# Moving eight of layer B's adaLN columns from the K/V products into the SSD output product

## The chip, the cores and the metric

The kernel runs on one core of one Trainium2 chip. The metric is the device time of one execution in microseconds (us); lower is better. A time is the median of several executions. One further execution is recorded by the hardware profiler; the profile and all queries of the trace come from that one.

## The reference, cut to what matters

The program is a two-layer decoder trunk for 256 tokens of width 2048, in float32. Layer A is a Mamba-2 (SSD) mixer, layer B a dilated-window attention. Each layer is

```
shift, scale, gate = split(silu(c) @ ada_w[layer] + ada_b[layer])       # adaLN, three vectors of 2048
h = x * (1 + scale) + shift
x = layer_norm(alpha * x + (1 + gate) * mixer(h)) * ln_g + ln_b
```

For layer A the mixer ends in `y @ out_w` with `y` 256 x 4096 and `out_w` 4096 x 2048: the "output product" below. After layer A the shared keys and values `x @ kv_w` (2048 x 6144) are made: the "K and V products". Layer B then forms its `h` with its own shift and scale, which need `c` alone, and multiplies it with `b_in_w`.

`ada_w` is 2048 x 6144 per layer. The kernel cuts it into 48 columns per layer (16 for each of shift, scale and gate), each a block of 128 x 2048 float32, 1 MB. A column is worked off without TensorE: the block is loaded and one VectorE instruction multiplies it with silu(c), laid out on every partition, and sums each row.

## The kernel before, in words

**Products.** Every large product is cut into weight pieces of 128 x 1024 float32 (512 KB). SP issues the load of a piece (`load_piece`, L93, tile `raw`, six buffers). ScalarE (ACT) rounds it to the fast matmul type (`split`, L99, tile `whi`, four buffers), VectorE (DVE) subtracts that from the original (L101, tile `wlo`, four buffers), and TensorE (PE) multiplies both parts with the split activations. So each piece passes SP, ACT, DVE and PE, and each engine works off its own instructions strictly in the order in which they were written into its queue.

**Output product** (L734 to L754). `tm_chunk` runs four chunks n = 0 to 3 of 512 output columns, 16 pieces each, for two halves of the tokens (b = 0, 1). Each matmul is one of L173 (high part by high part), L174 (low part of the weights) and L175 (low part of the activations). At the end of a chunk `residual` (L696 to L698, DVE) multiplies the sum by the gate, adds alpha * x and takes LayerNorm statistics, for each half. Chunk 3 also splits four pieces of the first V product (`first_weights`) in between. After it follow the LayerNorm's moments (L703 to L710) and normalisation (L720, ACT), the transposes (L766), and the copies of the transposed tiles (L769 on ACT, L770 on DVE).

**K and V products** (L808 to L821). First a V chunk (wv[4], 8 pieces), then twelve K tiles by `cm_wide` (4 pieces each, 48 in all; matmuls L149 and L152; each tile's sum is copied out by L156 on ACT and L157 on DVE), then three V chunks (wv[1], wv[3], wv[5], 24 pieces). Then comes layer B's `h` (L828, L829, L197, L198), the attention bias (load L835, use L868), the LayerNorm rows (tile `pT`, load L63, use L848) and layer B's input product.

**Columns in the background.** `queue(pool, cols)` (L267) puts one job per column into a list: a job issues the load of the next column (L244 on SP, tile `araw`, two buffers) and the dot of its own (L251 on DVE). `background(n, every)` (L106), called after each piece, adds n to a counter and runs a job for each full `every`. So a rate (1, 4) is one column for four pieces, (1, 2) one for two, (2, 5) two for five. `drain` (L279) runs what is left. Layer B's 48 columns are the list `cols1`: first 32 of scale and shift in turn, then 16 of gate. `pin` holds a dot back until a given earlier DVE instruction has been issued. The scheduler that writes the queues takes instructions in the order of the program, with each engine's readiness, so a job's place on DVE isn't exactly the place where it was called.

In before, the first 11 columns run in chunks 1 to 3 of the output product, at (1, 4) from 44 calls of `background` (the last four pieces of chunk 3 are split together and call it not). The other 37 run in the K and V products at (1, 2).

Of the kernel before, what the change touches and what calls it, by code (L numbers as in the profile page):

```python
# [21 lines left out]
KT = D // P  # L22
# [27 lines left out]
def trunk(ctx, tc, xT, x, c, par, cst, bias, lnrow, ada, wdt, win, wxs, wout, wk, wv, wbin, wbout, out):  # L50
# [11 lines left out]
    def bcast(dst, src, off=0):  # L62
        nc.sync.dma_start(dst, bass.AP(tensor=src.tensor, offset=src.offset + off,  # L63
                                       ap=[[0, P], [1, dst.shape[-1]]]))
# [22 lines left out]
    def rows(t, b):  # L87

        return t.rearrange("(j r) n -> r j n", r=2)[b]
# [42 lines left out]
    def cm_quad(src, ahi, alo, rate=(0, 1), k0=0):  # L132
        ps = acc_pair()
        for q in range(k0 // 2, KT // 2):
            cm_piece(src, q, ps, ahi, alo, k0=k0)
            background(*rate)
        return ps

    def cm_wide(src, dst, rate=(0, 1), moving=None):

        both, high = moving or (lambda kt: xp[:, kt], lambda kt: xhi[:, kt, :])
        ps = acc_pair()
        for q in range(KT // 4):
            hi, lo = (t.rearrange("p k n -> p (k n)").rearrange("p (k n) -> p k n", k=4)
                      for t in split(load_piece(src[q])))
            for k in range(4):
                kt = 4 * q + k
                for n in range(2):
                    T.matmul(ps[n], hi[:, k, n * P:n * P + P], both(kt), start=kt == 0, stop=False,  # L149
                             skip_group_check=True)  # L150
                for n in range(2):
                    T.matmul(ps[n][:, 0, :], lo[:, k, n * P:n * P + P], high(kt), start=False, stop=kt == KT - 1,  # L152
                             skip_group_check=True)
            background(*rate)
        for n in range(2):
            S.activation(dst[:, n, :], ps[n][:, 1, :], AF.Copy)  # L156
            V.tensor_tensor(dst[:, n, :], ps[n][:, 0, :], dst[:, n, :], op=ALU.add)  # L157

    def tiles(ps):
        return [ps[n // 2][:, n % 2, :] for n in range(4)]  # L160
# [17 lines left out]
    def tm_pair():  # L178
        return [mm.tile([P, 512], F32, name="acc") for _ in range(2)]

    def tm_chunk(src, ahi, alo, nk=KT, rate=(0, 1), k0=0, pre=None, split_end=0):

        ps = tm_pair()
        n = nk // 2 - split_end
        for q in range(k0 // 2, n):
            if pre:
                pre(q)
            tm_piece(src, q, ps, ahi, alo, k0, nk)
            background(*rate)
        held = [(q, split(load_piece(src[q]))) for q in range(n, nk // 2)]  # L190
        for b in range(2):
            for q, w in held:
                tm_mults(q, w, ps, ahi, alo, k0, nk, (b,))
        return ps
# [41 lines left out]
    def shift(i, kt):  # L236
        return mod[i][:, kt, 0:1]

    def scale(i, kt):
        return mod[i][:, kt, 1:2]  # L240

    def ada_load(pool, layer, kind, ct):
        raw = pool.tile([P, D], F32, name="araw", bufs=2)
        nc.sync.dma_start(raw, ada[layer, KIND.index(kind), ct])  # L244
        return raw

    def ada_dot(layer, kind, ct, raw):

        j = KIND.index(kind)
        with tc.issue_after(pin[0]) if pin[0] is not None else ExitStack():  # L250
            V.scalar_tensor_tensor(raw, raw, 1.0, cb_, op0=ALU.mult, op1=ALU.mult,  # L251
                                   accum_out=mod[layer][:, ct, j:j + 1])
# [14 lines left out]
    def queue(pool, cols):  # L267

        loaded = [ada_load(pool, *cols[0])]

        def step(i):
            raw = loaded.pop(0)
            if i + 1 < len(cols):
                loaded.append(ada_load(pool, *cols[i + 1]))
            ada_dot(*cols[i], raw)

        jobs.extend(lambda i=i: step(i) for i in range(len(cols)))

    def drain():  # L279
        while jobs:  # L280
            jobs.pop(0)()
# [8 lines left out]
    with ExitStack() as cA:  # L290
# [14 lines left out]
        with ExitStack() as cS:  # L305
# [38 lines left out]
            def xs_wide(g):  # L344

                xs[g] = p0.tile([P, 4, L], F32, name="xs")
                for w in range(2):
                    t = xs[g][:, 2 * w:2 * w + 2, :]
                    cm_wide(wxs[2 * g - 4 + w], t, rate=R, moving=(lambda kt: hp[:, :, kt, :], hh_))
                    for n in range(2):  # L350
                        conv(t[:, n, :], 4 * g + 2 * w + n, t[:, n, :])

            def product(kind, g, pre=None):
# [7 lines left out]
                if kind == "z":  # L361
                    ps = tm_chunk(src, hh_, hl_, rate=R, k0=k0, pre=pre)
                    if g not in sz:
# [5 lines left out]
                    return  # L369
                ps = cm_quad(src, hhi, hlo, rate=R, k0=k0)  # L370
                t = tiles(ps)
# [9 lines left out]
            with ExitStack() as c0:  # L381
# [42 lines left out]
                for row in ("b4:0. b6:0. h z2:0. b2:0 x1:0 h", "b2:1. x1:1. z1:0 z1:1. z4:0 h h",  # L424
# [3 lines left out]
                    for w in row.split():  # L428
                        if w == two:
                            n = -2 if sum(o[0] == -2 for o in order) == sum(o[0] == -1 for o in order) else -1  # L430
# [98 lines left out]
            px = pe = cS.enter_context(tc.tile_pool(name="px", bufs=2, reuse_waits="tile"))  # L529
            R = (1, 10)  # L530

# [133 lines left out]
        pn = cA.enter_context(tc.tile_pool(name="pn", bufs=1, reuse_waits="tile"))  # L665
# [47 lines left out]
        cols1 = [(1, kind, kt) for kt in range(KT) for kind in ("scale", "shift")] + \  # L713
# [19 lines left out]
        jobs.append(lambda: gate_out(0))  # L733
        for n in range(4):  # L734
            ps = tm_chunk(wout[n], lambda kt: yhi[kt // 16][:, kt % 16, :], lambda kt: ylo[kt // 4][:, kt % 4, :],
                          nk=2 * KT, rate=(1, 4) if n else (1, 2),
                          pre={0: y_ahead, 3: first_weights}.get(n), split_end=4 if n == 3 else 0)
            if n == 0:
                drain()
                pin[0] = latest[-3].ins  # L740
                state[0] = 0
                queue(pn, cols1[:11])
            if n == 3:
                drain()
            gt = pn.tile([P, 512], F32, name="gt")
            bcast(gt, gated[0], 512 * n)
            for b in range(2):
                xr = pn.tile([P, 512], F32, name="xr", bufs=2)
                nc.sync.dma_start(xr, rows(x, b)[:, 512 * n:512 * n + 512])
                residual(n, ps[b], b, (gt, u[b][:, 512 * n:512 * n + 512]), xr)  # L750
                if n == 3:
                    norm.append(moments(b, 4))
                    normalise(b, 0, 256)
                    normalise(b, 256, 512)  # L754
# [29 lines left out]
    with ExitStack() as cL:  # L784
        pl = cL.enter_context(tc.tile_pool(name="pl", bufs=3))

        vps = [tm_pair(), tm_pair()]
        for b in range(2):
            for kt in range(4):
                tile4 = x_tile(kt, (b,))  # L790
            for n in range(1, 4):
                normalise(b, 512 * n, 512 * n + 512)
            for i, w in enumerate(first_v):
                if b and i == 2:
                    x_tile(4)
                    x_tile(5)
                tm_mults(i // 2, w, vps[i % 2], hx, lx, 0, KT, (b,))
        for q in range(2, KT // 2):
            if q < KT // 2 - 1:
                x_tile(2 * q + 2)  # L800
                x_tile(2 * q + 3)
            for j in range(2):
                w = split(load_piece(wv[2 * j][q]), after=tile4.ins if q == 2 else None)
                tm_mults(q, w, vps[j], hx, lx, 0, KT, range(2))
        for g in range(2):
            evict_v(0, g, vps[g])

        R = (1, 2)  # L808
        pin[0] = latest[-1].ins
        with tc.issue_after(tile4.ins):  # L810
            state[0] = 0
            queue(pl, cols1[11:])
            jobs.append(lambda: gate_out(1))
            evict_v(0, 2, tm_chunk(wv[4], hx, lx, rate=R))
            for hq in range(2):
                for g in range(NG):
                    kv[hq, g] = place(3 + 3 * hq + g, [P, 4, L])
                    for w in range(2):
                        cm_wide(wk[2 * (2 * g + hq) + w], kv[hq, g][:, 2 * w:2 * w + 2, :], rate=R)
            for g in range(NG):  # L820
                evict_v(1, g, tm_chunk(wv[1 + 2 * g], hx, lx, rate=R))  # L821
            drain()
            late = latest[-1].ins

        ada_bias(1, slice(0, KT), slice(0, 2))
        for kt in range(KT):
            t = pl.tile([P, L], F32, name="htmp")
            S.activation(t, xhi[:, kt, :].bitcast(F32), AF.Identity, bias=shift(1, kt), scale=scale(1, kt))  # L828
            V.scalar_tensor_tensor(t, xlo[:, kt, :].bitcast(F32), scale(1, kt), t, op0=ALU.mult, op1=ALU.add)  # L829
            split_act(xhi[:, kt, :], xlo[:, kt, :], t)  # L830
# [7 lines left out]
    R = (0, 1)  # L838
# [269 lines left out]
```

## Time and profile before

| | us |
|---|---|
| median of 3 runs | 1255.48 |
| lowest, highest | 1254.13, 1258.44 |
| the profiled execution | 1254.31 |
| its span in the trace | 1252.5 |
| mean granted TensorE clock | 0.998 of full |

In the rows of the profile a group reads: line, engine, operation, output <- input, shape, count, then busy time, mean ns of one, idle time ahead of it and what ended most of that. In a row of a timeline the first number is the start and the second the duration, both in us; the bracket at the end holds the engine's idle time before it and the instruction that ended it. A row of the chain has start, time and what was then last. PEld is the loading of weights into TensorE, which overlaps the matmuls.

### The profile page before, as it was taken

What the parts mean: (1) busy time and instruction counts of PE and PEld (TensorE: products, weight loads), DVE (VectorE), ACT (ScalarE), POOL (GpSimd) and SP (SyncE); (2) the same over time, 40 slices, a digit from 0 to 9 for tenths busy, and PEclk for the clock granted to TensorE, in tenths of its full rate; (3) what the DMA queues carried; (4) which work ended last, traced back from release to release, by engine and by line L of the source; (5) the groups of instructions that cost most, each with busy time, mean ns of one, the idle gap of its engine ahead of it and who ended that gap; (6) DMA issues with size and microseconds to landing.
All of it is one profiled execution on the core that took longest, in us unless ns stands there. A gap on an engine that the chain in (4) does not pass through costs nothing.

```text
span 1252.5 us, 18746 instructions
## 1 busy us (share of the span) xinstructions
PE 1218.5 (97%) x7086; PEld 1042.7 (83%) x7086; DVE 1032.4 (82%) x1466; ACT 702.1 (56%) x1039; POOL 0.2 (0%) x4
## 2 busy tenths in 40 slices
PE   4999999999999999999999999999999999999997
PEld 4989998898888878788888788888888888888886
DVE  6999986999987989899777778879888866758777
ACT  3655577869588789653444444434445644445631
POOL 0000000000000000000000000000000000000000
PEclk9999999999999999999999999999999999999999
DMA  9999977677556546699898569989998774464741
GB/s 381 422 421 423 420 252 261 225 274 286 201 169 225 171 159 202 223 328 358 335 323 298 174 192 383 363 315 344 364 389 309 229 248 136 132 203 120 228 177 67
DMA packets 80586, 335.88 MB, mean 268 GB/s; under 512 B 9104, under 2 KB 9328, under 8 KB 67696
## 3 DMA queue, kind: packets, MB, share of 16 engines
q1 hardware_dynamic: 80496, 334.69, 73.9%
q8 instruction: 55, 0.90, 0.3%
q14 instruction: 35, 0.29, 0.1%
HBM read 332.47 MB, written 2.18 MB: 267 GB/s over the span
## 4 chain that ended last, share of the span: by engine, by line
PE 86%; DVE 5%; DMA 5%; issue 2%; ACT 1%; SPq 0%; DVEq 0%; ACTq 0%
PE acc L149 20%; PE acc L174 13%; PE acc L175 13%; PE acc L173 13%; PE acc L152 10%; PE acc L125 3%; PE acc L127 3%; PE acc L126 3%; DMA raw<-in_wk 2%; DVE wlo L101 1%; PE py L625 1%; DMA raw<-in_win 1%; DVE araw L251 1%; DMA araw<-in_ada 1%; DMA raw<-in_wv 1%
## 5 line engine op out<-in xcount | busy, mean ns | idle before, releaser
L99 ACT ACTIVATE whi<-raw 128x1024 fp32r<-128x1024 f32 x392 | 412.1, 1058 | 386.0 <-PE acc L175 151.4
L101 DVE TENSOR_TENSOR wlo<-raw,whi 128x1024 fp32r<-128x1024 f32 x392 | 473.5, 1221 | 145.3 <-ACT whi L99 141.1
L149 PE MATMUL acc<-actT,whi 128*128 128x512 f32 x1280 | 405.2, 397 | 0.0
L152 PEld LDWEIGHTS acc<-actT,wlo 128*128 128x128 f32 x1280 | 238.9, 188 | 62.8 <-DVE wlo L101 8.2
L174 PE MATMUL acc<-wlo,actT 128*128 128x512 f32 x688 | 270.0, 392 | 0.6 <-DVE wlo L101 0.5
L173 PE MATMUL acc<-whi,actT 128*128 128x512 f32 x688 | 266.6, 394 | 1.2 <-ACT actT L681 1.2
L152 PE MATMUL acc<-actT,wlo 128*128 128x256 f32 x1280 | 253.7, 280 | 4.5 <-DVE wlo L101 3.7
L251 DVE SCALAR_TENSOR_TENSOR araw<-araw,cb__72 128x2048 f32<-128x2048 f32 x96 | 219.3, 2285 | 9.5 <-DMA araw<-in_ada 9.3
L149 PEld LDWEIGHTS acc<-actT,whi 128*128 128x128 f32 x1280 | 195.8, 189 | 0.4
L175 PE MATMUL acc<-whi,actT 128*128 128x512 f32 x432 | 168.8, 391 | 0.0
L174 PEld LDWEIGHTS acc<-wlo,actT 128*128 128x128 f32 x688 | 129.3, 188 | 28.5 <-DVE wlo L101 2.8
L173 PEld LDWEIGHTS acc<-whi,actT 128*128 128x128 f32 x688 | 128.8, 188 | 27.2 <-ACT actT L681 1.7
L125 PE MATMUL acc<-actT,whi 128*128 128x256 f32 x384 | 108.9, 288 | 17.6 <-ACT actT L414 17.5
L126 PE MATMUL acc<-actT,whi 128*128 128x256 f32 x384 | 109.5, 287 | 0.0
L127 PE MATMUL acc<-actT,wlo 128*128 128x256 f32 x384 | 107.3, 287 | 1.2 <-DVE wlo L101 1.2
L175 PE MATMUL acc<-whi,ylo 128*128 128x512 f32 x256 | 100.7, 393 | 0.0
L175 PEld LDWEIGHTS acc<-whi,actT 128*128 128x128 f32 x432 | 81.1, 188 | 16.6
L125 PEld LDWEIGHTS acc<-actT,whi 128*128 128x128 f32 x384 | 74.3, 194 | 18.6 <-ACT actT L414 17.7
L126 PEld LDWEIGHTS acc<-actT,whi 128*128 128x128 f32 x384 | 75.1, 196 | 0.3
L127 PEld LDWEIGHTS acc<-actT,wlo 128*128 128x128 f32 x384 | 73.9, 196 | 1.6 <-DVE wlo L101 1.6
L175 PEld LDWEIGHTS acc<-whi,ylo 128*128 128x128 f32 x256 | 48.1, 188 | 9.7
L583 ACT ACTIVATE seg<-cbc,cumT 128x128 f32<-128x128 f32 x128 | 41.2, 389 | 5.0 <-PE py L625 4.9
(257 smaller groups left out, 1061.7 us busy)
## 6 DMA issues: line engine op xcount, KB each, us to landing
araw<-in_ada SPq DMA_DIRECT2D x96, 1024.0 KB, 7.3
raw<-in_win SPq DMA_DIRECT2D x112, 512.0 KB, 6.1
raw<-in_wout SPq DMA_DIRECT2D x64, 512.0 KB, 5.2
raw<-in_wbin SPq DMA_DIRECT2D x64, 512.0 KB, 4.2
raw<-in_wxs SPq DMA_DIRECT2D x48, 512.0 KB, 4.5
raw<-in_wv SPq DMA_DIRECT2D x48, 512.0 KB, 5.9
raw<-in_wk SPq DMA_DIRECT2D x48, 512.0 KB, 8.0
cbc<-cumd SPq DMA_DIRECT2D x16, 512.0 KB, 5.1
```

Of the source, the lines that this page charges most:

```text
L99: copied.append(S.activation(hi, raw, AF.Copy))
L101: latest.append(V.tensor_tensor(lo, raw, hi.bitcast(F32), op=ALU.subtract))
L125: T.matmul(o, hi[:, k, c_], ahi[:, kt, :], start=first, stop=False, skip_group_check=True)
L126: T.matmul(o, hi[:, k, c_], alo[:, kt, :], start=False, stop=False, skip_group_check=True)
L127: T.matmul(o, lo[:, k, c_], ahi[:, kt, :], start=False, stop=kt == k1 - 1, skip_group_check=True)
L149: T.matmul(ps[n], hi[:, k, n * P:n * P + P], both(kt), start=kt == 0, stop=False, skip_group_check=True)
L152: T.matmul(ps[n][:, 0, :], lo[:, k, n * P:n * P + P], high(kt), start=False, stop=kt == KT - 1, skip_group_check=True)
L173: T.matmul(o, h_, hi[:, k, :], start=kt == k0, stop=False, skip_group_check=part)
L174: T.matmul(o, h_, lo[:, k, :], start=False, stop=False, skip_group_check=part)
L175: end = T.matmul(o, l_, hi[:, k, :], start=False, stop=kt == k1 - 1, skip_group_check=part)
L251: V.scalar_tensor_tensor(raw, raw, 1.0, cb_, op0=ALU.mult, op1=ALU.mult, accum_out=mod[layer][:, ct, j:j + 1])
L583: S.activation(seg[:, hh, b, :], cbc[:, hh, b, :], AF.Relu, bias=cumT[:, b, h0 + hh:h0 + hh + 1], scale=-1.0)
```

## The change

The first 19 instead of 11 of layer B's columns go to the output product, at two columns for five pieces instead of one for four. The remaining 29 instead of 37 go to the K and V products, at two for five pieces instead of one for two. Of the 19, the 44 calls in chunks 1 to 3 start 17, and the `drain` ahead of chunk 3's residual the other two.

```
-                          nk=2 * KT, rate=(1, 4) if n else (1, 2),
+                          nk=2 * KT, rate=(2, 5) if n else (1, 2),
...
-                queue(pn, cols1[:11])
+                queue(pn, cols1[:19])
...
-        R = (1, 2)
+        R = (2, 5)
...
-            queue(pl, cols1[11:])
+            queue(pl, cols1[19:])
```

## The prediction

> **What bounds the kernel now.** I read the page first: busy times, the chain by engine, the costliest groups, the transfer issues.
>
> ```profile
> span 1252.5 us, 18746 instructions
> PE 1218.5 (97%) x7086; PEld 1042.7 (83%) x7086; DVE 1032.4 (82%) x1466; ACT 702.1 (56%) x1039; POOL 0.2 (0%) x4
> PE 86%; DVE 5%; DMA 5%; issue 2%; ACT 1%; SPq 0%; DVEq 0%; ACTq 0%
> L101 DVE TENSOR_TENSOR wlo<-raw,whi 128x1024 fp32r<-128x1024 f32 x392 | 473.5, 1221 | 145.3 <-ACT whi L99 141.1
> L251 DVE SCALAR_TENSOR_TENSOR araw<-araw,cb__72 128x2048 f32<-128x2048 f32 x96 | 219.3, 2285 | 9.5 <-DMA araw<-in_ada 9.3
> araw<-in_ada SPq DMA_DIRECT2D x96, 1024.0 KB, 7.3
> raw<-in_wout SPq DMA_DIRECT2D x64, 512.0 KB, 5.2
> ```
>
> PE holds 86% of the chain that ends last, and is busy 97% of the span. No column is added or dropped: 96 dots (L251) of 2.285 us and 96 transfers of 1 MB stay. Only where PE waits can the time change. So I listed PE by stretches of 15 us, over the output product (about 574 to 704) and over the K and V products (776 to 980). The columns are: PE busy and matmuls in the window, PEld, DVE, ACT, POOL, granted clock, DMA share, GB/s.
>
> ```profile
> 590.00:605.00 15.00, 15.00 (x68) 12.43 (x67) 9.79 (x11) 6.27 (x6) 0.00 (x0) 1.00 1.03 417
> 650.00:665.00 15.00, 15.00 (x68) 12.43 (x67) 10.82 (x13) 8.01 (x8) 0.00 (x0) 1.00 0.93 341
> 785.00:800.00 15.00, 15.00 (x88) 13.05 (x87) 12.76 (x16) 6.63 (x10) 0.00 (x0) 1.00 0.90 342
> 860.00:875.00 15.00, 13.91 (x79) 11.49 (x78) 13.92 (x17) 7.20 (x10) 0.00 (x0) 1.00 0.93 346
> 935.00:950.00 15.00, 14.94 (x64) 11.67 (x64) 12.95 (x12) 8.07 (x9) 0.00 (x0) 1.00 0.93 364
> ```
>
> Where eight of the columns go, PE is full: 68 matmuls in both windows of the output product. Where they leave, PE has holes: 79 matmuls at 860 against 88 at 785, 64 at 935 against 68 at 650.
>
> **The gain: the holes of the K and V products.** Their size comes from the stage's ends in the PE timeline: first K matmul, first of wv[1], first of layer B's input product; then the pitch of a K piece in the chain of waits, and the pitch of a 512-column matmul (first and last of 28 in a row).
>
> ```profile
> 775.85 0.62 PE L149 MATMUL acc<-actT,whi 128*128 128x512 f32 x2
> ...
> 912.92 0.63 PE L173 MATMUL acc<-whi,actT 128*128 128x512 f32 x2
> ...
> 979.72 0.61 PE L149 MATMUL acc<-actT,whi 128*128 128x512 f32 x2
> ...
> 840.09 0.46 PE acc L149 x2
> 840.56 0.23 PE acc L152 x2
> ...
> 617.81 0.39 PE L174 MATMUL acc<-wlo,actT 128*128 128x512 f32 x1
> 623.93 0.39 PE L174 MATMUL acc<-wlo,actT 128*128 128x512 f32 x1
> ```
>
> One k-tile of a K piece takes 0.465 + 0.23 = 0.695 us, a piece (four of them) 2.78, the 48 pieces 133.5. The stage takes 912.92 - 775.85 = 137.07: 3.5 lost. A 512-column matmul takes (623.93 - 617.81) / 27 = 0.2267; the 24 V pieces of 12 are 65.3, the stage takes 66.80: 1.5 lost. Together 5.0. The holes that one can see singly make about 4.4.
>
> What makes them is in the DVE and ACT timelines and the chain around 843:
>
> ```profile
> 842.80 0.66 ACT L156 ACTIVATE s<-acc 128x256 f32<-128x256 f32 x2 [4.82 <-PE acc L152]
> 843.35 3.12 ACT L99 ACTIVATE whi<-raw 128x1024 fp32r<-128x1024 f32 x3
> 843.22 0.76 DVE L157 TENSOR_TENSOR s<-acc,s 128x256 f32<-128x256 f32 x2 [2.56 <-ACT s L156]
> 845.59 2.28 DVE L251 SCALAR_TENSOR_TENSOR araw<-araw,cb__72 128x2048 f32<-128x2048 f32 x1
> 847.80 2.36 DVE L101 TENSOR_TENSOR wlo<-raw,whi 128x1024 fp32r<-128x1024 f32 x2
> 848.34 7.95 DMA raw<-in_wk
> ```
>
> The eviction of a K tile (L156 on ACT, L157 on DVE) waits for PE's last matmul of the tile. ACT and DVE are held 4.82 and 2.56 us on it with little split ahead; then come three copies in a row, and on DVE a dot of 2.28 us between the subtractions. The subtraction PE needs stands behind that dot at 847.80. The dot also frees the araw buffer whose refill stands on SP ahead of the next weights, which land 7.95 us later.
>
> The changed kernel's engine orders show both causes shrink. Now dots come every second piece, then two for every five: per four pieces DVE has 4 x 1.14 (pitch of subtractions) + 1.6 x 2.2 + 0.76 = 8.8 us instead of 9.7, in a tile's 11.1. The bytes are 4 x 0.524 + 1.6 x 1.049 = 3.78 MB in 11.1 us, 339 GB/s, instead of 4.19 MB, 377. The rows above moved 346 to 417. And L156 and L157 stand four (L157 three or four) pieces behind the tile's last split in the queues instead of one in the late tiles, so splits are ready while they wait. I take the 4.4 as gone (bounds 0 and -5.0): **-4.4 us**.
>
> **The price: two hand-overs of the output product.** The residual of a chunk (L696 to L698, two token halves) waits on DVE for PE's end of the chunk. What is split by then carries PE over it. In before, between chunks 1 and 2:
>
> ```profile
> 616.62 1.28 DVE L696 TENSOR_TENSOR u<-acc,gt 128x512 f32<-128x512 f32 x2
> 617.82 1.28 DVE L697 SCALAR_TENSOR_TENSOR u<-xr,u 128x512 f32<-128x512 f32 x2
> 619.02 1.28 DVE L698 BATCH_NORM_STATS2 st<-u 128x6 f32<-128x512 f32 x2
> 620.21 2.34 DVE L101 TENSOR_TENSOR wlo<-raw,whi 128x1024 fp32r<-128x1024 f32 x2
> 622.48 2.28 DVE L251 SCALAR_TENSOR_TENSOR araw<-araw,cb__72 128x2048 f32<-128x2048 f32 x1
> ```
>
> The residual takes 620.21 - 616.62 = 3.6 us, and three pieces of the next chunk are split ahead of it: 8 us of PE work. It cost PE nothing: in the rows above the 28 matmuls from 617.81 to 623.93 run at full pitch. In the changed order **one** piece is ahead of it, at both hand-overs:
>
> ```
> before, 1 to 2:  ... split 195, 196, 197 | residual | split 198, 199, dot
> after,  1 to 2:  ... split 195 | residual | split 196, dot, split 197
> after,  2 to 3:  ... split 211 | residual | split 212, dot, split of V piece, split 214, dot, split 215
> ```
>
> (195 and 211 are the first pieces of chunks 2 and 3.) Let PE begin the new chunk at 0. The residual's first product starts 0.43 us behind the start of the last matmul that it waits for, as these rows of the last chunk show:
>
> ```profile
> 703.72 0.40 PE L175 MATMUL acc<-whi,ylo 128*128 128x512 f32 x1
> 704.15 0.69 DVE L696 TENSOR_TENSOR u<-acc,gt 128x512 f32<-128x512 f32 x1 [1.08 <-PE acc L175]
> 704.87 0.69 DVE L697 SCALAR_TENSOR_TENSOR u<-xr,u 128x512 f32<-128x512 f32 x1
> ```
>
> The first half's last matmul starts 4 x 0.227 = 0.9 ahead of the boundary, so the residual starts at -0.48 and ends at 3.1. Split 196 is done at 3.1 + 1.23 = 4.33. PE, through with 195 at 2.72, does two products with whi alone and wants wlo at 3.18: **1.15 lost**. The dot runs to about 6.5, split 197 is done at 7.7; PE wants it at 3.18 + 1.15 + 2.72 = 7.05: **0.65 lost**. At 2 to 3 the first loss is the same; then a dot and a V piece stand ahead of 214: 4.33 + 2.2 + 1.14 + 1.23 = 8.9 against 7.05: **1.85**; and 215, behind one more dot, is done at 8.9 + 2.2 + 1.23 = 12.3 against 7.05 + 1.85 + 2.72 = 11.6: **0.7**. Behind that DVE catches up, since a piece and 0.4 dot cost it 1.14 + 0.9 = 2.0 of PE's 2.72. The sum is 1.8 + 3.7 = 5.5. If the residual's six instructions run 0.72 apart as single ones do (704.15 and the next at 704.87) instead of 0.6, it is 0.7 more at each: 6.9. If only the first loss of each counted, because the dots came late for want of their bytes, it is 2.3. I take **+5.5**.
>
> The transfers there rise: a chunk is 16 x 0.524 MB of weights and 6.4 x 1.049 MB of columns instead of 4 x 1.049, with the residual's operands (0.8 MB) 15.9 MB in 43.5 us, 365 GB/s; chunk 3 with its V pieces some 400. The row at 590 moved 417 with PE full, so I add nothing; if that cover is gone it is the last rival.
>
> [...]
>
> **Two small terms.** In the changed order L696 of the second half stands ahead of the last instruction of the first half's moments (L710):
>
> ```profile
> 702.91 0.16 DVE L710 SCALAR_TENSOR_TENSOR e0nb<-e0mv,e0y 128x1 f32<-128x1 f32 x1
> 703.10 1.80 ACT L720 ACTIVATE u<-u,e0nb,e0y 128x256 f32<-128x256 f32 x3 [0.62 <-DVE e0nb L710]
> 705.30 0.50 PE L173 MATMUL acc<-s,actT 128*128 128x512 f32 x1 [0.97 <-ACT actT L769]
> ...
> PE acc L173 <- ACT actT L769: 1.4, 2, 1.0
> ```
>
> L710 then comes at 704.15 + 0.72 = 704.87, 1.96 later, and with it L720. Behind L720 stand transposes, L769 and PE's first V product at 705.30. But one normalisation fewer stands between in ACT's order, and of the waits of 1.4 in this stretch (last row) the part behind the first is then over already. Between 0 and +1.96; **+0.4**. Second, SP issues the attention bias (L835) and the LayerNorm rows after ten pieces of layer B's weights instead of eight:
>
> ```profile
> 987.28 0.96 DVE L868 SCALAR_TENSOR_TENSOR bi<-bs 128x384 f32<-128x384 f32 x3 [1.87 <-DMA bs<-in_bias]
> 989.33 1.29 DVE L848 TENSOR_TENSOR u<-u,pT 128x512 f32<-128x512 f32 x2 [1.09 <-DMA pT<-in_lnrow]
> ```
>
> DVE waits for them by 1.87 and 1.09 with three splits ahead. Some 2.4 us later (two issues at the pace of PE's pieces, less what is already queued) the cover falls short by a little: between 0 and +2.5, **+0.4**.
>
> **Sum:** -4.4 + 5.5 + 0.4 + 0.4 = **+1.9 us**. The profiled execution took 1254.31 us (span 1252.5 and 1.8 around it), 1.2 below the median 1255.48. So the profiled one should read 1256.2, the median 1257.4. I forecast **1257**.
>
> **Rivals.**
> (a) *The hand-overs cost as computed, the holes stay (slower).* The cause of the holes could be the loop of two araw buffers through SP (dot, refill, weights behind it), not the place of L156. For it: the 7.95 us transfer in the chain right behind a dot; the cadence there, a tile each 11.57 us, is what 4.19 MB need at 362 GB/s. Against: 339 GB/s of need now, and V holes at a dot rate of one in two too. Half the gain kept: +1.9 + 2.2 to + 4.4, so 1259.6 to 1261.8. Chance 0.22.
> (b) *The hand-overs cost little (faster).* Place: DVE between two chunks. If the residual ran ahead of the chunk's end, or PE kept a deeper reserve than one piece, 5.5 falls to at most 1.5; then 1255.5 - 4.4 + 0.8 + 0 to 1.5 = 1251.9 to 1253.4. It decides when the reserve at the chunk's end is two pieces (5.4 us) or more, since split 196 is done at 4.33. For it: PE ran through all three hand-overs in before. Against: DVE works in order, and the order has one. Chance 0.13, a third of it beyond 0.3%.
> (c) *The change moves nothing:* dots are 0.1 per piece rarer or 0.15 more frequent, and each hole keeps its size: 1255.5. Against: the dot rate is what differs between the window at 590, which is full, and the one at 860, which isn't. Chance 0.03.
> (d) *Transfers bind in the output product.* If no more than the 362 GB/s of the K stage can be moved steadily, chunks 1 and 2 take 15.9 MB / 362 = 43.9 us instead of 43.5 and chunk 3 (20 pieces and 6 or 7 columns, 17.6 MB) 48.6: 5.9 more, of which six raw buffers (3.1 MB, 8.7 us of reserve) and the hand-over stalls themselves hide about half: +1.9 + 3 = 1260.4. [...] Against: 417 at 590 to 605. Chance 0.10.
>
> **How the numbers follow.** Forecast 0.52, (a) 0.22, (b) 0.13, (c) 0.03, (d) 0.10. About 0.3% (3.8 us: below 1251.7 or above 1259.2) is what a measurement of this kernel can tell from no change. Faster: a third of (b), and a little for what I have overlooked, as the far end of the forecast's bounds (gain 5.0, price 2.3 and nothing else: 1252.8) does not reach there: 0.07. Slower: (a), (d), and a tenth of the forecast (its small terms at their upper ends are +3.7 more, the price's is +1.4): 0.36. Same: 0.57. The range runs from 1252.3, inside (b), to (a)'s upper end, 1262; outside it lie some 0.05 of (b) and the tails.
>
> **What would show it.** Right: PE waits on wlo (L174, by L101) some 2.7 us behind each start of chunks 2 and 3, sums 1.8 and 3.7; the K stage in 134 us instead of 137.07, V in 65.5; a tile each 11.1 us instead of 11.57; PE waits between 700 and 710 and at 1005 within half a us of before. Wrong: no PE wait in 600 to 680 (b); holes of the same size behind dots in 845 to 945 (a); PE waits released by raw or whi in 640 to 700 (d).

## The result and the profile after

| | median us | lowest to highest | runs |
|---|---|---|---|
| before | 1255.61 | 1253.43 to 1258.44 | 15 |
| changed | 1258.43 | 1255.97 to 1262.12 | 15 |

The ratio is 1.0023, interval 1.0013 to 1.0033: the change makes the kernel 2.8 us slower (1.6 to 4.1). The forecast was 1257.

The profiled execution of the changed kernel took 1259.62 us, its span is 1257.8, so 5.3 more than the profiled execution of before. Some of that was there ahead of the change: PE reaches the output product at 525.1 us instead of 523.0 in a part where both programs are the same. Of these 2.1 us, 1.5 are a stretch near 469 us in which the matmuls run at half speed (see the last section). Executions differ by that much, which is why the comparison below goes by stages and not by the clock of the span.

First the stretches of the output product and of the K and V products, to be set against those of before. The columns are the same.

```profile
620.00:635.00 15.00, 13.54 (x59) 10.57 (x58) 15.00 (x16) 5.31 (x5) 0.00 (x0) 1.00 0.79 307
635.00:650.00 15.00, 15.00 (x67) 12.40 (x67) 12.59 (x13) 6.37 (x6) 0.00 (x0) 1.00 1.02 406
665.00:680.00 15.00, 12.09 (x51) 9.04 (x50) 15.00 (x16) 5.19 (x5) 0.00 (x0) 1.00 0.65 228
710.00:725.00 15.00, 12.64 (x50) 9.42 (x50) 10.07 (x38) 8.98 (x16) 0.00 (x0) 0.89 0.38 143
860.00:875.00 15.00, 15.00 (x88) 13.09 (x87) 12.11 (x14) 5.85 (x7) 0.00 (x0) 1.00 0.92 335
935.00:950.00 15.00, 15.00 (x68) 12.40 (x67) 11.77 (x11) 6.66 (x8) 0.00 (x0) 1.00 0.84 302
```

The holes have changed places. At 860 and 935 PE is full now. At 620 and 665, where chunks 2 and 3 begin, it has 59 and 51 matmuls of 68, while DVE is busy for all 15 us: DVE is what is late there. Transfers are not: the window between the two holes moves 406 GB/s with PE full, those with a hole 307 and 228. The window at 710 has a hole, as before has there, and, as the only one of these, a granted clock below 1 (0.89).

Next the waits: PE's from 615 to 680, then PEld's from 770 to 985, where the list of the changed kernel is empty and that of before has 4.3 and 1.9:

```profile
PE acc L174 <- DVE wlo L101: 4.4, 5, 1.4
```

```profile
PEld acc L152 <- DVE wlo L101: 4.3, 6, 1.4
PEld acc L174 <- DVE wlo L101: 1.9, 5, 0.5
```

The five waits of 4.4 us can be read one by one. Here are DVE and PE of the changed kernel around the start of chunk 2 (its first matmul stands at 619.16):

```profile
614.95 1.23 DVE L101 TENSOR_TENSOR wlo<-raw,whi 128x1024 fp32r<-128x1024 f32 x1 [3.13 <-ACT whi L99]
618.68 1.37 DVE L696 TENSOR_TENSOR u<-acc,gt 128x512 f32<-128x512 f32 x2 [2.51 <-PE acc L175]
...
621.17 1.28 DVE L698 BATCH_NORM_STATS2 st<-u 128x6 f32<-128x512 f32 x2
622.37 1.21 DVE L101 TENSOR_TENSOR wlo<-raw,whi 128x1024 fp32r<-128x1024 f32 x1
623.49 2.28 DVE L251 SCALAR_TENSOR_TENSOR araw<-araw,cb__72 128x2048 f32<-128x2048 f32 x1
625.71 2.35 DVE L101 TENSOR_TENSOR wlo<-raw,whi 128x1024 fp32r<-128x1024 f32 x2
```

```profile
623.63 0.50 PE L174 MATMUL acc<-wlo,actT 128*128 128x512 f32 x1 [1.13 <-DVE wlo L101]
...
626.98 0.50 PE L174 MATMUL acc<-wlo,actT 128*128 128x512 f32 x1 [0.33 <-DVE wlo L101]
...
669.20 0.50 PE L174 MATMUL acc<-wlo,actT 128*128 128x512 f32 x1 [1.13 <-DVE wlo L101]
...
673.68 0.50 PE L174 MATMUL acc<-wlo,actT 128*128 128x512 f32 x1 [1.45 <-DVE wlo L101]
...
677.03 0.50 PE L174 MATMUL acc<-wlo,actT 128*128 128x512 f32 x1 [0.33 <-DVE wlo L101]
```

DVE stands idle for 2.51 us in front of the residual because PE has not ended the chunk, although the next piece has been ready for its split since 616.22, when ACT ended its copy. That split begins only at 622.37, and PE waits for it; the one after it stands behind the dot and makes the second wait. The last three rows are the same at the start of chunk 3 (its first matmul stands at 664.74), where a dot and a V piece stand in between.

The table sets the stages side by side. A chunk is measured from its first L175 to the next chunk's, chunk 3 to its last; "LayerNorm" is from there to the first K matmul; K and V are as in the prediction (785.86, 919.61 and 985.04 in the changed kernel). "Rest" runs from there to the end of the span.

| stage, us | before | changed | difference | forecast |
|---|---|---|---|---|
| chunk 1, with its end | 43.55 | 44.05 | +0.5 | 0 |
| chunk 2, with the hand-over to it | 43.52 | 45.58 | +2.1 | +1.8 |
| chunk 3, with the hand-over to it | 42.84 | 46.43 | +3.6 | +3.7 |
| LayerNorm, first V product, wv[4] | 72.13 | 74.01 | +1.9 | +0.4 |
| K tiles | 137.07 | 133.75 | -3.3 | -4.4 with V |
| wv[1], wv[3], wv[5] | 66.80 | 65.43 | -1.4 | |
| rest | 272.78 | 272.76 | 0.0 | +0.4 |

In the changed kernel the first L175 of chunks 2 and 3 comes one matmul later in its piece than in before. That makes the row of chunk 1 0.2 too high and that of chunk 3 0.2 too low; set against before matmul by matmul, PE loses 0.3, 2.1 and 3.8 us in chunks 1, 2 and 3. The waits in the rows of PE (1.46 and 2.91 for chunks 2 and 3) are smaller, because a wait is counted from the end that the profile models for the matmul before it. By the starts of the matmuls the five losses are 1.29 and 0.49, then 1.29, 1.61 and 0.50, together 5.2. The rest, 0.14 behind each wait, is a slower pitch of the next few matmuls (0.34 instead of 0.227 us for the first).

### The profile page after: what moved, and what is told of

Its sections match the earlier page's. It is cut to its first block, busy times and chain, and to the rows that moved or that the text cites. A ratio compares the mean times of both kernels' runs of the same rounds, so it can differ in the third digit from the quotient of the medians.

```text
span 1257.8 us, 18729 instructions
## 1 busy us (share of the span) xinstructions
PE 1219.8 (97%) x7086; PEld 1045.3 (83%) x7086; DVE 1032.6 (82%) x1466; ACT 703.9 (56%) x1039; POOL 0.2 (0%) x4
## 4 chain that ended last, share of the span: by engine, by line
PE 83%; DMA 7%; DVE 6%; issue 2%; ACT 1%; SPq 1%; DVEq 0%; ACTq 0%
PE acc L149 22%; PE acc L174 11%; PE acc L175 11%; PE acc L173 11%; PE acc L152 11%; PE acc L125 3%; PE acc L127 3%; PE acc L126 3%; DMA pT<-in_lnrow 2%; DMA raw<-in_wout 2%; DMA raw<-in_win 2%; DVE wlo L101 1%; PE py L625 1%; DVE araw L251 1%; DMA xr<-in_x 1%
## 5 line engine op out<-in xcount | busy, mean ns | idle before, releaser
L149 PE MATMUL acc<-actT,whi 128*128 128x512 f32 x1280 | 406.3, 398 | 0.0
L152 PEld LDWEIGHTS acc<-actT,wlo 128*128 128x128 f32 x1280 | 240.2, 189 | 59.6 <-DVE wlo L101 4.1
L152 PE MATMUL acc<-actT,wlo 128*128 128x256 f32 x1280 | 253.6, 280 | 3.4 <-DVE wlo L101 3.4
L251 DVE SCALAR_TENSOR_TENSOR araw<-araw,cb__72 128x2048 f32<-128x2048 f32 x96 | 219.2, 2284 | 9.6 <-DMA araw<-in_ada 9.4
L149 PEld LDWEIGHTS acc<-actT,whi 128*128 128x128 f32 x1280 | 196.5, 189 | 0.4
L175 PE MATMUL acc<-whi,actT 128*128 128x512 f32 x432 | 168.7, 391 | 0.0
L175 PE MATMUL acc<-whi,ylo 128*128 128x512 f32 x256 | 100.8, 394 | 0.0
L175 PEld LDWEIGHTS acc<-whi,actT 128*128 128x128 f32 x432 | 81.1, 188 | 16.9
L175 PEld LDWEIGHTS acc<-whi,ylo 128*128 128x128 f32 x256 | 48.1, 188 | 9.5
```

The source lines that it names most:

```text
L175: end = T.matmul(o, l_, hi[:, k, :], start=False, stop=kt == k1 - 1, skip_group_check=part)
```

## The experiments

Each ratio is to runs of the kernel before on the same chip. "Stage" numbers are measured as in the table.

**after_again.** The changed kernel, unedited, for one more profile.

> The changed kernel once more, for a second profile. Theory: the waits are set by the order of the instructions, so they recur: 1.3 + 0.5 us at the start of chunk 2, 1.3 + 1.6 + 0.5 at the start of chunk 3, about 1.9 between chunk 3 and the first V product, none in the K tiles. The half-speed matmuls at 714 to 718 us (0.42 instead of 0.227 apart) recur too if PE's idle time ahead of them brings them. Rival: the half speed is a chance event of that one execution and is not there again; then this stage is 2 us shorter.

It took 1262.38 us in its one run, so that no ratio can be given. The waits recur to 0.02 us: chunks 2 and 3 take 45.57 and 46.44, K and V 133.75 and 65.43. The half speed at the first V product does not recur: this stage takes 72.40 instead of 74.01, so of its +1.9 only +0.3 belongs to the order of instructions. But a half-speed stretch stands at another place of this execution, behind a wait of 2.01 us:

```profile
1024.42 0.50 PE L152 MATMUL acc<-actT,wlo 128*128 128x256 f32 x2 [2.01 <-DVE wlo L101]
...
1026.74 1.05 PE L149 MATMUL acc<-actT,whi 128*128 128x512 f32 x2
1027.60 0.63 PE L152 MATMUL acc<-actT,wlo 128*128 128x256 f32 x2
1028.02 1.01 PE L149 MATMUL acc<-actT,whi 128*128 128x512 f32 x2
1028.87 0.41 PE L152 MATMUL acc<-actT,wlo 128*128 128x256 f32 x2
1029.11 0.62 PE L149 MATMUL acc<-actT,whi 128*128 128x512 f32 x2
```

A pair of L149 and a pair of L152 take 1.28 us here (1026.74 to 1028.02) instead of 0.695. The window from 1025 to 1030 has a granted clock of 0.66. So the rival was right about this term: it is a chance event, which came both times behind waits of PE that sum to about 2 us. The rest of the longer span lies ahead of the change, in chunk 0: 52.57 us instead of 50.66, by a wait of PE that one profile of this kernel has and the other has not.

**late_residual.** The residuals of chunks 1 and 2, with the loads of their rows of x, move behind the first three splits of the next chunk.

```
+        def held_back(q, also=None):
+            if q == 3 and waiting:
+                with tc.issue_after(latest[-1].ins):
+                    waiting.pop(0)()
...
+            if n in (1, 2):
+                waiting.append(join_chunk)
```

> The changed kernel, but the residuals of chunks 1 and 2 are issued behind the first three splits of the next chunk. Theory (hand-overs): the waits at the starts of chunks 2 and 3, 5.2 us by their gaps and 5.9 by the shift of PE's work, go; 1258.4 becomes 1252.5 to 1253.5, ratio to the kernel before 0.998. Rival (transfers bind there at over 400 GB/s): the splits come no earlier, the same time is lost at raw, 1257 to 1259, ratio 1.002.

1253.61 us, ratio 0.9981 (0.9969 to 0.9992). Chunks 2 and 3 take 43.52 and 42.84, to the hundredth what they take in before. No wait of PE from 590 to 700 is left. The same bytes move in less time: 421 and 388 GB/s in the windows at 620 and 665, where the changed kernel moved 307 and 228. So the loss is the place of the residual in DVE's queue, and neither the bytes nor the sum of DVE's work.

**late_two.** As late_residual, with two splits ahead (`q == 2`).

> The changed kernel with the residuals of chunks 1 and 2 behind the first two splits of the next chunk instead of three (or one, as in the change). Theory (the reserve at the boundary sets the wait): two pieces are 5.4 us of PE work, the residual ends at 3.1 and the next split at 4.33, or 6.5 where a dot stands in between: 0 to 0.6 us at the first hand-over, 0 to 0.3 at the second, where three pieces cost nothing and one piece cost 2.1 and 3.6. Chunk 2 44.1 us, chunk 3 43.0, the whole 1253.5 to 1254.5, ratio 0.9985. Rival (the waits come from elsewhere, and three pieces only happened to avoid them): half the loss stays, chunk 2 44.6 and chunk 3 44.6.

1253.92 us, ratio 0.9986 (0.9973 to 1.0000). Chunk 2 takes 44.46 and chunk 3 43.34. With one, two and three pieces ahead the first hand-over loses 2.1, 0.9 and 0 us, the second 3.8, 0.5 and 0. At the first one a dot stands within the residual here (DVE runs L251 from 622.03 to 624.24, between L696 and L697); I take that to be the difference between the two, but no run shows it. Expected were 0 to 0.6 and 0 to 0.3, a few tenths too low. Chunk 2 alone, 44.46, lies nearer the rival's 44.6 than the 44.1 expected; chunk 3, 43.34, speaks against the rival.

**ln_order.** The second half's residual of chunk 3 goes behind the first half's moments, as in before.

```
-                residual(n, ps[b], b, (gt, u[b][:, 512 * n:512 * n + 512]), xr)
+                with tc.issue_after(last_moment[-1].ins) if last_moment else ExitStack():
+                    residual(n, ps[b], b, (gt, u[b][:, 512 * n:512 * n + 512]), xr)
```

> The changed kernel, but the second half's last residual is issued behind the last instruction of the first half's moments, as before. Theory: the wait of 1.5 us on the normalisation and the half-speed stretch behind it go: 1.9 us less, 1256.5, ratio 1.001; PE's first V product about 1.6 us after the last matmul of chunk 3 instead of 2.75. Rival: the wait moves to the second half's moments and nothing is won: 1258.4, ratio 1.002.

1257.84 us, ratio 1.0025 (1.0015 to 1.0035): not told apart from the changed kernel. PE's first V product comes 1.06 us after chunk 3 instead of 2.75, but a wait of 0.7 on a transposed tile (L771 of this kernel) follows:

```profile
PE acc L173 <- ACT actT L770: 0.9, 2, 0.4
PE aux L767 <- DVE xtmp L771: 0.7, 1, 0.7
```

The stage takes 72.18, against 72.13 in before and 72.40 in the execution of the changed kernel without half speed there. Expected was 1.9; 0.2 is what the order was worth. My expectation had charged the half speed to it.

**late_and_ln.** Both edits.

> Both edits in the changed kernel. Theory: what is left of the change is the gain in the K and V products, 4.5 us: 1251 to 1251.5, ratio 0.9965, faster than the kernel before. Rival (transfers): 1256.5, ratio 1.001.

1252.28 us, ratio 0.9978 (0.9969 to 0.9987): faster than before, and within its interval of late_residual. By stages the gain in K and V is whole: 133.75 and 65.43. But by the median 2.8 us are won, not the 4.5 expected, and 0.9965 lies outside the interval; where the rest went stays open.

**wout_part.** The changed kernel with `R = (1, 2)` in the K and V products.

> 19 columns in the output product as in the change, but the 29 others in the K and V products at the old rate of one for two pieces (so they end some 22 pieces earlier). Theory: the hand-over losses stay whole (+5.9 with the normalisation's +1.9), and the holes of the K tiles stay, since the evictions stand one piece behind their tile again, except in the last 22 pieces, where no dots are left: about 1260.5, ratio 1.004. Rival (what made the holes was the sum of dots and bytes): the same, since rate and bytes per tile are the old ones; what would speak against both is a K stage without holes.

1261.59 us, ratio 1.0047 (1.0031 to 1.0063). The hand-overs are as in the change (45.61, 46.45). The K tiles take 136.30: most of the holes are back. wv[1] to wv[5], where no dot is left, take 65.46. So in the changed kernel the holes of the K tiles go by the lower rate in the K products, not by anything that happens in the output product. The copies out of PSUM stand in the same places as in before: the traces have DVE's copy of a tile 4 splits behind the tile's last one at first, then 3 and 2, and 1 in the last seven of the twelve tiles; in the changed kernel it is 4 or 3 throughout.

**kv_part.** Before, with the K and V products' part of the change; eight columns in between are left out and their entries set to zero, so that 8 MB less are loaded and the output is not the reference's.

```
-        R = (1, 2)
+        R = (2, 5)
...
-            queue(pl, cols1[11:])
+            for _, kind, kt in cols1[11:19]:
+                j = KIND.index(kind)
+                V.memset(mod[1][:, kt, j:j + 1], 0.0)
+            queue(pl, cols1[19:])
```

> The kernel before with 11 columns in the output product at one for four, and 29 in the K and V products at two for five; the eight columns in between (cols1[11:19]) are left out, their entries are set to zero, so 8 MB are not loaded and the output is not the reference's. Theory: no hand-over losses and no holes: 1255.6 less 4.5 = 1251, ratio 0.9965. Rival (the changed kernel's K stage is free only because the bytes went elsewhere and something else then binds): cannot be told by this one alone; a ratio above 0.999 would speak against the gain.

1251.76 us, ratio 0.9963 (0.9949 to 0.9977). K and V take 133.75 and 65.43, the chunks 43.52 and 42.84. The gain of 4.7 us is whole without the price. kv_part and wout_part together, -0.37% and +0.47%, make +0.10%; the change has +0.23%. The sum counts a part of the gain twice: wout_part has 29 dots in the K and V products instead of 37, and its K and V stages are already 2.1 us below those of before, 0.17%.

**late_evict.** Before, with all its columns and rates; the K tiles' copies out of PSUM go behind the first three splits of the next tile.

```
+            if q == behind and evictions:
+                evictions.pop(0)()
...
+                with tc.issue_after(copied[-1].ins) if behind else ExitStack():
                     S.activation(dst[:, n, :], ps[n][:, 1, :], AF.Copy)
+                with tc.issue_after(latest[-1].ins) if behind else ExitStack():
                     V.tensor_tensor(dst[:, n, :], ps[n][:, 0, :], dst[:, n, :], op=ALU.add)
```

> The kernel before with all its columns and rates, but each K tile's two copies out of PSUM are issued behind the first three splits of the next tile. Theory (place of the eviction in the queues): the holes of the K tiles, 3.5 us, go: 1252, ratio 0.997. Rival (dots and the loop dot, refill, weights through two araw buffers): the holes stay, a tile each 11.57 us: 1255.6, ratio 1.000.

1251.95 us, ratio 0.9968 (0.9956 to 0.9980). The K tiles take 133.75 with the old rate of dots:

```profile
845.00:860.00 15.00, 15.00 (x89) 13.09 (x88) 13.29 (x13) 6.52 (x8) 0.00 (x0) 1.00 0.98 388
860.00:875.00 15.00, 15.00 (x88) 13.09 (x87) 14.61 (x19) 7.74 (x11) 0.00 (x0) 1.00 0.94 363
935.00:950.00 15.00, 14.94 (x65) 11.70 (x65) 14.77 (x13) 6.13 (x6) 0.00 (x0) 1.00 0.91 341
```

PE is full at 845 and 860 with 388 and 363 GB/s moved, more than before moved there with holes (355 and 346). So neither the dots nor their bytes made the holes of the K tiles by themselves; the copies' place in the queue did. In the trace DVE's copy now stands 3 splits behind all tiles but the first and the last (4 and 1). The V hole at 935 stays (wv[1], wv[3] and wv[5] take 66.79), since that part was not edited.

**araw3.** Before, with three araw buffers in the K and V products.

```
-        raw = pool.tile([P, D], F32, name="araw", bufs=2)
+        raw = pool.tile([P, D], F32, name="araw", bufs=3 if three[0] else 2)
```

> The kernel before with three araw buffers instead of two in the K and V products, so that SP does not hold the weights behind the refill of a column. The evictions stand one or two pieces behind their tile, in the late tiles one, as before. Theory (place of the eviction): the late holes stay, at most 1 us won: 1254.5 to 1255.6, ratio 0.9995. Rival (the loop through two araw buffers): the holes go, 1252, ratio 0.997.

1254.67 us, ratio 0.9990 (0.9979 to 1.0001). The K tiles take 136.22: 0.85 of 3.3 us is won, the other holes stay. The third buffer also moved some evictions in the queue (DVE's copy stands 1 split behind in the last five tiles instead of the last seven), so that even the 0.85 can't be laid to the buffer alone. The loop through two buffers is at most a small part.

**best_pt** and **evict_pt.** Late_and_ln and late_evict, with each LayerNorm row of layer B's input product loaded one piece ahead of its first use.

```
-        if b == 0 and i == 0:
+        if i < 0:
             t = pc2.tile([P, 1024], F32, name="pT", bufs=1)
...
+            return
...
-    jobs.extend(lambda n=n, b=b, i=i: weigh(n, b, i) for n in range(4) for i in range(2) for b in range(2))
+    jobs.extend(lambda n=n, b=b, i=i: weigh(n, b, i) for n in range(4) for b, i in ((0, -1), (0, 0), (1, 0), (0, 1), (1, 1)))
```

> The changed kernel with late residuals and the old LayerNorm order, and each LayerNorm row of layer B's input product is loaded one piece ahead of its first use instead of together with it. Theory: the wait of 0.9 to 1.9 us at about 1015, where DVE stands at these rows ahead of a split, goes, and with it the chance of a half-speed stretch behind it: 1251, ratio 0.9965. Rival: the rows are then late at another place, 1252.3 as without the edit, ratio 0.998.

> The kernel before with late evictions of the K tiles, and the LayerNorm rows loaded one piece ahead. Theory: in the late_evict run this wait was not there in the profiled execution, so at most 0.5 us is won: 1251.5 to 1252, ratio 0.9965. Rival: the shifted rows cost a split its place, 1253, ratio 0.998.

best_pt took 1252.90 us, ratio 0.9969 (0.9957 to 0.9981); evict_pt 1253.62, ratio 0.9984 (0.9974 to 0.9995). Neither is told apart from its parent. In best_pt DVE still waits for a row, by 3.58 us, and PE by 1.46 behind it:

```profile
1014.28 0.69 DVE L866 TENSOR_TENSOR u<-u,pT 128x512 f32<-128x512 f32 x1 [3.58 <-DMA pT<-in_lnrow]
1014.89 1.22 DVE L101 TENSOR_TENSOR wlo<-raw,whi 128x1024 fp32r<-128x1024 f32 x1
```

The edit missed: with one buffer a row's load has to wait for the last use of the row before it, so that a job in between gains little. Of the versions that do all the work late_evict has the lowest time, 1251.95; late_and_ln, best_pt and late_evict can't be told apart.

## Why the prediction was right

**Gain in K and V (-4.4).** Measured -4.7, and alone (kv_part) -0.37%, 4.6 us. The explanation had two parts, rarer dots and the place of the copies, and I said that both shrink. The runs put it more sharply: with the copies moved and the dots kept the K holes go (late_evict), with the old rate of dots and the copies left they mostly stay (wout_part, 136.30). The rate matters because at the lower one the scheduler puts the copies three or four pieces behind in all tiles. The V holes come and go with the dots (66.80 at one for two, 65.43 at two for five, 65.46 with none in wout_part); what about the dots makes them was not tried. One reading was off without effect: the rows of before that the 339 GB/s were set against moved 341 to 417, not 346 to 417.

**Price of the hand-overs (+5.5).** Measured +5.9 (2.1 and 3.8). By the starts of the matmuls the first loss at either hand-over is 1.29 against 1.15 worked out; the others are 0.49 against 0.65, and 1.61 and 0.50 against 1.85 and 0.7. That makes 5.2; the slower restart behind the five waits, which the working did not have, adds 0.7. So the sum came out closer than its parts, by luck. late_residual and late_two confirm the mechanism, and the reserve as its measure.

**Missed: chunk 1 (+0.3).** I looked at the hand-overs to chunks 2 and 3 only. At the one ahead of chunk 1's work a dot now stands in front of the residual on DVE, waits 0.96 us for its column, and delays the residual and the splits behind it; PE begins with the first of these at 592.04, when it has just ended, and falls back by 0.3 us:

```profile
584.96 2.29 DVE L251 SCALAR_TENSOR_TENSOR araw<-araw,cb__72 128x2048 f32<-128x2048 f32 x1 [0.96 <-DMA araw<-in_ada]
587.18 1.28 DVE L696 TENSOR_TENSOR u<-acc,gt 128x512 f32<-128x512 f32 x2
```

In other versions of the changed kernel this stage loses between 0.1 (late_residual) and 0.9 us (ln_order). No run was made for it, so the cause rests on the rows.

**LayerNorm order (+0.4).** Worth +0.3 (72.40 against 72.13) in the execution without a half-speed stretch. PE's first V product comes 1.2 us later behind chunk 3 (2.75 against 1.58), as the reordering of L710 had it, and the stage regains 0.9 of that. The first profile has +1.9, by 1.6 us of half speed, which I had not thought of.

**Layer B's rows (+0.4).** The rest of the span takes the same, 272.76 against 272.78. The wait near 1020 was 1.32 in one and 2.01 in the other profile of the changed kernel, against 0.33 + 0.38 in before; so +0.6 or more in these waits. Set against before matmul by matmul, PE's lag grows by 0.3 us over that wait in the first profile (from 5.3 to 5.6) and falls back by 0.3 later; in the second it grows by 2.6, half-speed stretch included, and the rest of the span takes 275.0. The sign that was to show this term and the one before, PE's waits within half a us of before, did not hold: 2.4 instead of 1.6 us between 700 and 760, and these.

**Sum.** By stages without the half speed: 0.3 + 2.1 + 3.8 + 0.3 - 4.7 + 0 = +1.8, forecast +1.9, measured +2.8 (1.6 to 4.1). That the first two agree to 0.1 is luck in part: the missed 0.3 of chunk 1 and 0.4 of the hand-overs are made up by 0.3 more of gain in K and V and by the two small terms, which came out 0.5 lower together. The waits that the change adds, of up to 2 us, now and then bring a half-speed stretch of about 1.6 us. For the waits ahead of the first V product this should be about three executions in ten, 0.5 us on average, an estimate from the windows in the last section; the rest is not shown, and lies within the interval.

**Rivals.** (a), the holes stay through the loop of two buffers: refuted by the K stage of 133.75, and araw3 shows the loop as a minor part in before too. (b), hand-overs at little cost: needed a reserve of two pieces. The change has one; and late_two shows that two would not have been enough, since it loses 0.9 + 0.5. (c), that nothing moves: the interval of the ratio leaves out 1, and both parts of the forecast show in the stages. (d), transfers bind: 406 GB/s with PE full in the changed output product, and late_residual moves the same bytes without loss.

## What to carry to other kernels

In these runs an instruction that waits for the end of a matmul group cost nothing while three prepared pieces stood ahead of it in its engine's queue (late_residual: chunks 2 and 3 take 43.52 and 42.84 us, as in before). With one or two ahead it cost (2.1 and 3.8 us with one, 0.9 and 0.5 with two), roughly, its length (3.6 us of residual and the dots around it) less what these pieces gave PE to do. So look in the issued order for how many pieces stand ahead of each such instruction; a change of background work moves this number although it edits neither of the two. Here moving two residuals, or the copies of twelve tiles, by a few places in the queue was worth more (late_residual 4.8 us below the changed kernel, late_evict at 0.9968 of before) than moving eight columns of work between stages (1.0023).

## What the runs showed of the hardware

Behind waits of PE of some 2 us the matmuls sometimes run at half speed for 3.4 us: one of 512 columns takes 0.42 instead of 0.227 us. In the changed kernel the granted clock is 0.98 from 710 to 715 and 0.68 from 715 to 720, so 1.7 us of clock are missing, which is 3.4 us at half.

```profile
715.00:720.00 5.00, 5.00 (x18) 3.80 (x17) 4.09 (x20) 4.03 (x7) 0.00 (x0) 0.68 0.91 369
```

The same wait of 1.49 us, with 0.44 more soon behind it, was there in after_again, late_residual, late_two and wout_part with no such stretch. So the length alone doesn't decide. Within each trace that has several stretches ahead of its end, they begin whole multiples of 3.413 us apart (in the changed kernel at 25.27, 469.01 and 714.77: 443.74 us or 130 of them, then 245.76 or 72). So I cut the traces into windows of that length. Their borders have no fixed place in the program: the matmul at which PE's wait near 467 us ends starts 1.18 us behind a border in before (467.08, border at 465.90) and 2.07 behind one in the changed kernel (467.66, 465.59). Here are two neighbouring windows of the changed kernel and then two of after_again, around the same waits:

```profile
711.35:714.77 3.42, 1.50 (x7) 0.76 (x7) 2.42 (x6) 1.70 (x4) 0.00 (x0) 1.00 0.10 14
714.77:718.18 3.41, 3.41 (x10) 2.55 (x11) 2.57 (x15) 2.44 (x6) 0.00 (x0) 0.50 0.88 327
```

```profile
711.41:714.82 3.41, 2.96 (x14) 2.11 (x12) 1.86 (x10) 1.06 (x1) 0.00 (x0) 1.00 0.10 40
714.82:718.24 3.42, 1.94 (x10) 1.41 (x11) 3.28 (x13) 2.92 (x7) 0.00 (x0) 1.00 0.39 105
```

In the first, PE is idle for 1.92 us of one window, and the next one has the granted clock 0.50. In the second a border falls between, the windows have 0.45 and 1.48 us of idle PE, and the clock stays at 1. Between the first 30 us and the last 20 of all thirteen traces there are nine stretches at half clock. Seven stand behind windows with 1.92 to 2.08 us of idle PE, and no such window is without one; one stands behind 1.90 and one behind 1.66. Six other windows with 1.67 to 1.90, and all others with less, had none. So in these thirteen traces more than 1.90 us of idle PE within one window had half speed behind it each time, and less than 1.66 never. Between these bounds the windows of the changed kernel with most are those with 2.07 (465.59 to 469.01) and 1.92 us (711.35 to 714.77), each with the clock 0.50 in the next; behind the one that follows, with 1.44 (670.39 to 673.81), it is 1.00. One wait of 2.08 us near 467 us is in all thirteen traces and has half clock behind it in five. In before it is divided by the border at 465.90, the two windows have 0.89 and 1.18 us of idle PE, and the clock is 1.00 in both and in the next. If the borders fall at random, it should lie whole in one window in (3.41 - 2.08) / 3.41 = 39% of the executions, an estimate; five of thirteen is 38%. In the same way the waits of 1.49 and 0.44 us, 2.37 from the start of the first to the end of the second, give 31%.
